# A ring of eleven buffers for the gathered expert rows of a kernel's last 256 tokens

## The chip, the core and the metric

The kernel runs on one core of a Trainium2 chip, as one launch. The metric is the device time of that launch in microseconds (us); lower is better. Engines are named as in the profile: PE is TensorE (PEld its weight loads), DVE is VectorE, ACT is ScalarE, POOL is GpSimd, SP is SyncE, whose queue issues the plain DMAs. Row gathers (indirect DMAs) are issued by POOL.

## The reference, cut to what matters

One decoder layer on 1024 tokens of width 1024: a token mixer with three branches, then a feed-forward layer that picks, for each token, 8 heads x 16 experts out of 16384, and a last norm. Only the expert layer bears on this change:

```
def chunk(xc):                                   # 128 tokens
    qh = (xc @ w_q).reshape(Ct, H, 2, PEER_QDIM // 2)
    s = jnp.einsum("nhad,akd->nhak", qh, sub_keys)
    top_s, top_i = lax.top_k(s, K)
...
    eidx = jnp.take_along_axis(cand_idx, pos, axis=-1)
    gate = jax.nn.softmax(best_s, axis=-1)
    ug = u_tab[eidx]
    vg = v_tab[eidx]
    hpre = jnp.einsum("nd,nhkd->nhk", xc, ug)
    act = gate * jax.nn.gelu(hpre, approximate=False)
    return jnp.einsum("nhk,nhkd->nd", act, vg)
```

So a token reads 128 rows of `u_tab` and 128 rows of `v_tab`, each of 1024 float32 numbers.

## The kernel before, in words

The 1024 tokens are cut into four parts of 256 (two tiles of 128 tokens each). All parts go through the mixer, the norm and the routing. Then the expert layer is computed in two ways.

Parts 1 and 2 (512 tokens) are done densely: 128 iterations, each for 128 experts, on PE. An iteration loads 512 KB of the u table (`uraw`) and 512 KB of the v table (`vraw`), splits both into two float16 halves (`us`, `vs`; high half on ACT, low half on DVE, line 212), multiplies the tokens with u (`g`, 24 matmuls, line 256), takes GELU, multiplies by the gates (`ge`, DVE line 1411), splits the result (`ac`, DVE line 212) and multiplies it with v (`acc`, 18 matmuls, line 1418; every fourth iteration 24 more into `g`). `gemm1` runs three iterations ahead.

Parts 0 and 3 (tiles 0, 1 and 6, 7) gather their rows instead, in `gather_tile`. For column c of a tile's 128 expert numbers, POOL issues one indirect DMA that brings one row for each of 128 tokens, a tile of 128 x 1024 float32 (512 KB), called `u6_5` for tile 6, column 5. DVE multiplies it with the normed tokens `gh2` and sums into column c of `hpre` (line 1144); 128 columns make the u phase of a tile. Then `act` is formed, and in the v phase each gathered `v` row is multiplied by its `act` column and added to `gacc` (line 1154), one after the other, since each addition reads the sum of the one before. Tiles 6 and 7 run beside the dense iterations, and what is left of them runs after these.

A gathered row sits in a buffer from its issue until DVE has used it. Tiles 0 and 1 use the tag `rows` alone, with RB = 5 buffers. `gather_tile` takes its own tiles from the same five: `gh2` for the whole u phase, `gacc` from shortly before the v phase to the end. So four of the five are left for rows. Tiles 6 and 7 (the last part) take their rows through `late_rows`, which goes round a ring of RB + 4 = 9 places: five from `rows`, then four that are the halves of two tiles of the tag `hT` (two buffers of 128 x 2 x 1024; they held the part's normed tokens, which are no longer needed by then). Such a half shows up under the name `rr_u` or `rr_v` in the profile, the other rows as `u` or `v`. A tile of `hT` comes free when both halves have been used. With nine places and eight free buffers, the fifth place of a round shares its buffer with the first of the same round.

The order of instructions on each engine is fixed when the kernel is built: a scheduler puts what is ready, by its own estimate, in order of priority, and each engine then runs its list in that order and waits where data is missing. A buffer that comes free at another moment therefore moves instructions on POOL, DVE, PE, ACT and SP.

The tag `o0`, `o1`, `o2` (pool `wk`, one buffer each) holds a part's three branch outputs. For the last part it also serves, through `WT`, the norm's rows, the top-16 lists `ts` (`o2`) and the one-hot tables of the routing (`oneh0` in `o0`, `oneh1` in `o1`, lines 1061 to 1066). The routing of tile 7 is still using `oneh0` and `oneh1` when tile 6 begins to gather.

Of the kernel before, what the change touches and what calls it, by code (L numbers as in the profile page):

```python
# [10 lines left out]
F32 = mybir.dt.float32  # L11
# [18 lines left out]
RB, WB, AT, ZB, TB = 5, 4, 8, 2, 3  # L30

T = 1024
D = 1024
# [36 lines left out]
def trunk(ctx: ExitStack, tc: tile.TileContext, a: dict, out: bass.AP):  # L70
# [11 lines left out]
    wk = ctx.enter_context(tc.tile_pool(name="wk", bufs=1))  # L82
# [988 lines left out]
    def rows(name):  # L1071
        return gat.tile([128, D], F32, tag="rows", name=name, bufs=RB)

    taken = [0, None]

    def late_rows(name):

        j = taken[0] % (RB + 4)
        taken[0] += 1
        if j < RB:  # L1080
            return rows(name)
        if (j - RB) % 2 == 0:
            taken[1] = htp.tile([128, 2, D], F32, tag="hT", name=f"rr_{name}")
        return taken[1][:, (j - RB) % 2]

    marks = []
    seen = [0]
# [459 lines left out]
```

## Time and profile before

| | us |
|---|---|
| median of 3 runs | 3650.54 |
| lowest, highest | 3646.55, 3655.01 |
| the profiled execution, its own time | 3644.86 |
| its span, first to last instruction | 3643.1 |

| stretch of the span, us | what runs |
|---|---|
| 2447 to 2743 | u phase of tile 6, beside dense iterations |
| 2743 to 3045 | v phase of tile 6, beside dense iterations |
| 3056 to 3340 | u phase of tile 7, beside dense iterations |
| 3341 to 3635 | v phase of tile 7; the last dense matmul ends at 3548 |

A row of the timeline gives start, duration, engine, line, operation, output <- inputs, a count, and in brackets the idle time of the engine just before it and what ended that. A row of the waits says who waited for whom, the sum, how often, and the longest. A row of the windows gives, for one stretch, the busy time of each engine (and its number of instructions), then the clock granted to PE, the busy share of the 16 DMA engines and the bytes moved per second. POOL's time for a gather is the time that it takes to issue it; the data lands later.

### The profile page before, as it was taken

To read this page: it belongs to the slowest core of one execution; us is meant where nothing else is said; L and a number is where in the kernel's file an instruction comes from. 1 tells how busy PE (TensorE), PEld (TensorE's weight loads), DVE (VectorE), ACT (ScalarE), POOL (GpSimd) and SP (SyncE) were. 2 spreads that over 40 slices of the span, in tenths; PEclk is the share of its full clock that TensorE was granted. 3 is DMA by queue.
4 is the path that set the end of the run, shared out by engine and by line. 5 is a ranking of instruction groups with operands and counts; after the bars stand their busy time and mean duration, and the time that the engine had idled before them with its cause. 6 is when DMAs were issued, how large, how long until landed. Compare 5 with 4: busy or idle time off the path is not lost.

```text
span 3643.1 us, 57457 instructions
## 1 busy us (share of the span) xinstructions
PE 3273.9 (90%) x20660; PEld 2192.5 (60%) x20660; DVE 3025.3 (83%) x7062; ACT 1594.5 (44%) x3162; POOL 1358.0 (37%) x1166
## 2 busy tenths in 40 slices
PE   7999999999987999999788889989999999999980
PEld 6887777777875778787566554534444444444430
DVE  6665689888899879889988777999988888997887
ACT  5776455553543564654456423243333333333311
POOL 0000002344332423332232334316665666775564
PEclk9999999999995889999576799999999999999995
DMA  8964857889976768987465899869999999999987
GB/s 303 340 223 142 297 189 253 306 293 345 349 258 199 260 227 297 333 307 253 135 228 179 294 365 314 288 192 357 366 359 321 347 331 353 383 377 340 335 281 249
DMA packets 358764, 1053.90 MB, mean 289 GB/s; under 512 B 35175, under 2 KB 107563, under 8 KB 354381
## 3 DMA queue, kind: packets, MB, share of 16 engines
q0 software_dynamic: 147456, 536.94, 41.8%
q1 hardware_dynamic: 211020, 513.29, 39.7%
q8 instruction: 162, 2.65, 0.3%
q14 instruction: 126, 1.02, 0.1%
HBM read 942.09 MB, written 108.00 MB: 288 GB/s over the span
## 4 chain that ended last, share of the span: by engine, by line
PE 37%; DVE 20%; DMA 16%; issue 13%; ACT 7%; POOL 6%; SPq 0%; POOLq 0%; DVEq 0%; ACTq 0%
DMA v<-in_peer_v_dram,gidx 7%; PE g L256 5%; PE pj_mg L256 4%; PE acc L1418 4%; POOL rr_v L1152 3%; DVE gacc L1154 3%; DMA d_G<-stage 3%; PE pj_r_hg L256 3%; POOL v L1152 2%; DVE u L1144 2%; DMA u<-in_peer_u_dram,gidx 2%; ACT stage L1217 2%; PE g L1418 2%; PE pj_wo L256 1%; DMA gt<-d_G 1%
## 5 line engine op out<-in xcount | busy, mean ns | idle before, releaser
L1152 POOL DMA_INDIRECT v<-in_peer_v_dram,gidx x398 | 518.6, 1303 | 731.3 <-DVE gacc L1154 447.5
L1142 POOL DMA_INDIRECT u<-in_peer_u_dram,gidx x399 | 488.7, 1225 | 676.9 <-DVE u L1144 398.4
L256 PE MATMUL g<-h,us 128*128 128x512 f16 x3072 | 695.0, 384 | 20.2 <-ACT p L1427 9.9
L1154 DVE SCALAR_TENSOR_TENSOR gacc<-v,act,gacc 128x1024 f32<-128x1024 f32 x398 | 508.9, 1279 | 115.7 <-DMA v<-in_peer_v_dram,gidx 112.8
L1418 PE MATMUL acc<-vs,ac 128*128 128x512 f16 x2304 | 536.3, 383 | 19.8 <-ACT ac L211 11.1
L1418 PEld LDWEIGHTS <-ac 128*128 128x128 f16 x3072 | 302.5, 99 | 398.9 <-issue 24.1
L256 PEld LDWEIGHTS <-us 128*128 128x128 f16 x3072 | 303.3, 99 | 392.1 <-issue 31.2
L1144 DVE SCALAR_TENSOR_TENSOR u<-u,gh 128x1024 f32<-128x1024 f32 x399 | 481.0, 1217 | 36.6 <-DMA u<-in_peer_u_dram,gidx 35.2
L256 PE MATMUL pj_mg<-hT,w_mg 128*128 128x256 f16 x2304 | 278.8, 277 | 12.4 <-ACT mg L884 6.5
L256 PEld LDWEIGHTS <-w_mg 128*128 128x128 f16 x2304 | 229.8, 101 | 43.3 <-issue 15.7
L1377 ACT ACTIVATE ge<-g 128x512 f32<-128x512 f32 x128 | 75.8, 592 | 367.5 <-PE g L256 360.7
L211 ACT ACTIVATE ac<-ge 128x512 f16<-128x512 f32 x128 | 80.0, 626 | 348.5 <-DVE ge L1411 313.4
L1152 POOL DMA_INDIRECT rr_v<-in_peer_v_dram,gidx x113 | 167.0, 1478 | 112.7 <-DVE gacc L1154 78.1
L1142 POOL DMA_INDIRECT rr_u<-in_peer_u_dram,gidx x113 | 168.3, 1490 | 96.8 <-DVE rr_u L1144 58.4
L211 ACT ACTIVATE vs<-vraw 128x1024 f16<-128x1024 f32 x128 | 133.3, 1046 | 139.6 <-DMA vraw<-in_peer_v_dram 139.5
L1418 PE MATMUL g<-vs,ac 128*128 128x512 f16 x768 | 178.4, 384 | 11.6 <-ACT ge L1377 8.8
L212 DVE SCALAR_TENSOR_TENSOR vs<-vraw,vs 128x1024 f16<-128x1024 f32 x128 | 155.7, 1219 | 20.0 <-ACT vs L211 19.5
L1217 ACT ACTIVATE stage<-gb 128x512 f32<-128x512 f32 x128 | 131.0, 1072 | 81.9 <-DMA d_G<-stage 40.4
L212 DVE SCALAR_TENSOR_TENSOR us<-uraw,us 128x1024 f16<-128x1024 f32 x128 | 155.9, 1218 | 7.9 <-ACT us L211 7.3
L256 PE MATMUL pb<-o,w_b 128*128 128x256 f16 x1152 | 142.7, 280 | 18.2 <-DMA w_b<-dw 9.9
L1214 PE MATMUL gb<-hot 128*128 128x128 f16 x512 | 126.3, 295 | 35.3 <-DVE hot L1211 20.8
L1411 DVE TENSOR_TENSOR ge<-ge,gt 128x256 f32<-128x256 f32 x256 | 98.1, 421 | 60.8 <-ACT ge L1377 30.3
(1145 smaller groups left out, 6556.7 us busy)
## 6 DMA issues: line engine op xcount, KB each, us to landing
uraw<-in_peer_uT_dram SPq DMA_DIRECT2D x128, 512.0 KB
vraw<-in_peer_v_dram SPq DMA_DIRECT2D x128, 512.0 KB
w_mg<-dw SPq DMA_DIRECT2D x72, 512.0 KB
d_G<-stage SPq DMA_DIRECT2D x32, 1024.0 KB
gt<-d_G SPq DMA_DIRECT2D x32, 1024.0 KB
w_r_hg<-dw SPq DMA_DIRECT2D x36, 512.0 KB
w_b<-dw SPq DMA_DIRECT2D x72, 256.0 KB
wr_mg<-in_wblk_dram SPq DMA_DIRECT2D x24, 512.0 KB
```

The source lines that it names most:

```text
L211: S.activation(hi, src, AF.Copy, scale=scale)
L212: V.scalar_tensor_tensor(lo, in0=src, scalar=scale, in1=hi, op0=ALU.mult, op1=ALU.subtract)
L256: P.matmul(ps, l[:, k, :], r[:, k, :], start=(i == 0), stop=(i == n - 1))
L1142: G.indirect_dma_start(out=ur, out_offset=None, in_=a["peer_u"], in_offset=bass.IndirectOffsetOnAxis(ap=idx[:, c:c + 1], axis=0))
L1144: V.scalar_tensor_tensor(ur, in0=ur, scalar=1.0, in1=h2, op0=ALU.mult, op1=ALU.mult, accum_out=hpre[:, c:c + 1])
L1152: G.indirect_dma_start(out=vr, out_offset=None, in_=a["peer_v"], in_offset=bass.IndirectOffsetOnAxis(ap=idx[:, c:c + 1], axis=0))
L1154: V.scalar_tensor_tensor(acc, in0=vr, scalar=act[:, c:c + 1], in1=acc, op0=ALU.mult, op1=ALU.add)
L1214: P.matmul(ps[:, n, :], hs[:, 0, :, n], hs[:, 2, :, n], start=True, stop=False)
L1217: S.activation(stage[0][:, :, m0:m0 + 4].rearrange("p i n -> p n i"), ps, AF.Copy, scale=SA / SGT)
L1377: S.activation(ge, ps, AF.Gelu, scale=1.0 / (SW * SH2))
L1411: V.tensor_tensor(gv, gv, gt[:, :, i % 8, :], op=ALU.mult)
L1418: P.matmul(ps, ac[:, x, t * 128:(t + 1) * 128], v[:, y, dh * 512:(dh + 1) * 512], start=start and n == 0, stop=stop and n == 2)
```

## The change

The ring of the last part gets eleven places, each with a buffer of its own: four of `rows` (RB - 1 instead of RB), the four halves of `hT` as before, and the three buffers `o0`, `o1`, `o2`, one row each. Nothing else is edited. Line numbers behind the edit grow by four (1144 becomes 1148, 1154 becomes 1158).

```diff
     def late_rows(name):
 
-        j = taken[0] % (RB + 4)
+        j = taken[0] % (RB + 6)
         taken[0] += 1
-        if j < RB:
+
+        j -= RB - 1
+        if j < 0:
             return rows(name)
-        if (j - RB) % 2 == 0:
+        if j >= 4:
+            return wk.tile([128, D], F32, tag=f"o{j - 4}", name=name, bufs=1)
+        if j % 2 == 0:
             taken[1] = htp.tile([128, 2, D], F32, tag="hT", name=f"rr_{name}")
-        return taken[1][:, (j - RB) % 2]
+        return taken[1][:, j % 2]
```

The scheduler turns this into other lists, from the start of tile 6 on. Three places follow; numbers at the end of a name are the scheduler's own.

First, POOL in the v phase of tile 7, about column 100. Before, column 97 is the fifth of its round and stands behind the four halves of `hT` that follow it in number:

```order
L1152 DMA rr_v7_98_36111<-in_peer_v_dram,gidx_7_35471 128x1024 x2
L1152 DMA rr_v7_100_36116<-in_peer_v_dram,gidx_7_35471 128x1024 x2
L1152 DMA v7_97_36108<-in_peer_v_dram,gidx_7_35471 128x1024
L1152 DMA v7_102_36121<-in_peer_v_dram,gidx_7_35471 128x1024
L1152 DMA v7_103_36124<-in_peer_v_dram,gidx_7_35471 128x1024
```

Now, the same place:

```order
L1156 DMA rr_v7_93_36116<-in_peer_v_dram,gidx_7_35481 128x1024 x2
L1156 DMA rr_v7_95_36121<-in_peer_v_dram,gidx_7_35481 128x1024 x2
L1156 DMA v7_97_36126<-in_peer_v_dram,gidx_7_35481 128x1024
L1156 DMA v7_98_36129<-in_peer_v_dram,gidx_7_35481 128x1024
L1156 DMA v7_99_36132<-in_peer_v_dram,gidx_7_35481 128x1024
L1156 DMA v7_100_36135<-in_peer_v_dram,gidx_7_35481 128x1024
```

The columns now stand in the order of their numbers, seven single rows and four halves in turn.

Second, DVE at the end of the dense part: `ac127` is the split of the last iteration's GELU, `vs126` and `vs127` those of its last v blocks, and `gacc_7<-v7_79` the use of column 79. Before:

```order
L212 SCALAR_TENSOR_TENSOR vs127_32985<-vraw127_32983,vs127_32985 128x1024
L1154 SCALAR_TENSOR_TENSOR gacc_7_35837<-v7_76_36049,act_7_35477,gacc_7_35837 128x1024
L1428 TENSOR_TENSOR acc7_22937<-acc7_22937,p7_123_4_32854 128x512
L1154 SCALAR_TENSOR_TENSOR gacc_7_35837<-v7_77_36052,act_7_35477,gacc_7_35837 128x1024
L1411 TENSOR_TENSOR ge127_32863<-ge127_32863,gt120_0_32624 128x256
L1411 TENSOR_TENSOR ge127_32863<-ge127_32863,gt120_16_32626 128x256
L1154 SCALAR_TENSOR_TENSOR gacc_7_35837<-v7_78_36055,act_7_35477,gacc_7_35837 128x1024
L212 SCALAR_TENSOR_TENSOR ac127_32990<-ge127_32863,ac127_32990 128x512
L1154 SCALAR_TENSOR_TENSOR gacc_7_35837<-v7_79_36058,act_7_35477,gacc_7_35837 128x1024
```

Now:

```order
L212 SCALAR_TENSOR_TENSOR ac127_32990<-ge127_32863,ac127_32990 128x512
L212 SCALAR_TENSOR_TENSOR vs125_32925<-vraw125_32923,vs125_32925 128x1024
L1158 SCALAR_TENSOR_TENSOR gacc_7_35851<-v7_101_36138,act_7_35487,gacc_7_35851 128x1024
L1158 SCALAR_TENSOR_TENSOR gacc_7_35851<-v7_102_36141,act_7_35487,gacc_7_35851 128x1024
L1158 SCALAR_TENSOR_TENSOR gacc_7_35851<-v7_103_36144,act_7_35487,gacc_7_35851 128x1024
L1158 SCALAR_TENSOR_TENSOR gacc_7_35851<-rr_v7_104_36147,act_7_35487,gacc_7_35851 128x1024 x2
L1158 SCALAR_TENSOR_TENSOR gacc_7_35851<-rr_v7_106_36152,act_7_35487,gacc_7_35851 128x1024 x2
L1158 SCALAR_TENSOR_TENSOR gacc_7_35851<-v7_108_36157,act_7_35487,gacc_7_35851 128x1024
L1158 SCALAR_TENSOR_TENSOR gacc_7_35851<-v7_109_36160,act_7_35487,gacc_7_35851 128x1024
L1158 SCALAR_TENSOR_TENSOR gacc_7_35851<-v7_110_36163,act_7_35487,gacc_7_35851 128x1024
L212 SCALAR_TENSOR_TENSOR vs126_32955<-vraw126_32953,vs126_32955 128x1024
L1158 SCALAR_TENSOR_TENSOR gacc_7_35851<-v7_111_36166,act_7_35487,gacc_7_35851 128x1024
```

The next row of that list is `vs127`, and the one behind it column 112. Behind `ac127` stood columns 79 to 127, 49 rows; now stand columns 101 to 127, 27 rows. The split `vs127`, ahead of column 76 before, is ahead of column 112 now.

Third, POOL at the end of the u phase of tile 6. Before:

```order
L1152 DMA rr_v6_3_35103<-in_peer_v_dram,gidx_6_34726 128x1024 x2
L1152 DMA rr_v6_5_35108<-in_peer_v_dram,gidx_6_34726 128x1024 x2
L1142 DMA u6_108_35033<-in_peer_u_dram,gidx_6_34726 128x1024
L1142 DMA u6_109_35036<-in_peer_u_dram,gidx_6_34726 128x1024
L1142 DMA u6_110_35039<-in_peer_u_dram,gidx_6_34726 128x1024
L1142 DMA u6_111_35042<-in_peer_u_dram,gidx_6_34726 128x1024
```

Now:

```order
L1156 DMA v6_6_35116<-in_peer_v_dram,gidx_6_34726 128x1024
L1156 DMA rr_v6_8_35122<-in_peer_v_dram,gidx_6_34726 128x1024 x2
L1146 DMA u6_107_35034<-in_peer_u_dram,gidx_6_34726 128x1024
L1146 DMA u6_97_35006<-in_peer_u_dram,gidx_6_34726 128x1024
L1146 DMA u6_118_35065<-in_peer_u_dram,gidx_6_34726 128x1024
L1146 DMA u6_108_35037<-in_peer_u_dram,gidx_6_34726 128x1024
L1156 DMA v6_1_35101<-in_peer_v_dram,gidx_6_34726 128x1024
L1146 DMA u6_119_35068<-in_peer_u_dram,gidx_6_34726 128x1024
```

Columns 97, 108 and 119 share the buffer `o1`, columns 107 and 118 `o0`: the first rows in `o0` and `o1` (columns 8 and 9) wait for the routing of tile 7 and are issued behind columns 38 and 49, and these two buffers stay behind until the phase ends, where they are used one row after the other.

## The prediction

> **What bounds the kernel now.** I read the page first, then the windows over the four phases of tiles 6 and 7, then the waits in them, then the timeline of the last 50 us.
>
> ```profile
> span 3643.1 us, 57457 instructions
> PE 3273.9 (90%) x20660; PEld 2192.5 (60%) x20660; DVE 3025.3 (83%) x7062; ACT 1594.5 (44%) x3162; POOL 1358.0 (37%) x1166
> ```
>
> The lists differ only from the start of tile 6 on, so the page's means say little; the stretches do. The windows below are the v phase of tile 6, the u phase of tile 7, the v phase of tile 7 beside the dense part, and what comes behind it. In each: length, then busy time of PE, PEld, DVE, ACT and POOL with their counts, the clock granted to PE, the DMA share and GB/s.
>
> ```profile
> 2757.00:3045.00 288.00, 285.45 (x1316) 129.02 (x1314) 247.23 (x263) 90.66 (x122) 172.66 (x118) 0.99 0.95 335
> 3060.00:3290.00 230.00, 227.46 (x1047) 102.67 (x1046) 211.55 (x344) 78.16 (x105) 169.04 (x112) 0.99 1.02 383
> 3350.00:3540.00 190.00, 181.31 (x829) 81.49 (x827) 156.69 (x167) 52.17 (x71) 113.35 (x80) 0.97 0.90 318
> 3540.00:3643.00 103.00, 8.29 (x39) 3.56 (x37) 75.92 (x89) 12.60 (x25) 52.57 (x43) 0.56 0.73 247
> ```
>
> Two things are to be seen. While dense iterations run, PE is busy 95 to 99% of the time, so that stretch can't shrink; the only time to win is the last 95 us, when PE is done and rows are still coming. And POOL issues a row each 230 / 112 = 2.05 us in the u phase of tile 7, but only each 288 / 118 = 2.44 and 190 / 80 = 2.38 us in the two v phases, with the DMA engines at 335 and 318 GB/s instead of 383. Why, the waits say: the first fence is the v phase of tile 6, the second the u phase of tile 7, the third and fourth the last two windows.
>
> ```profile
> POOL v L1152 <- DVE gacc L1154: 45.6, 14, 6.1
> POOL rr_v L1152 <- DVE gacc L1154: 45.4, 20, 5.5
> DVE gacc L1154 <- DMA v<-in_peer_v_dram,gidx: 37.6, 12, 5.3
> ```
>
> ```profile
> POOL rr_u L1142 <- DVE rr_u L1144: 21.3, 11, 5.8
> ```
>
> ```profile
> POOL v L1152 <- DVE gacc L1154: 34.5, 14, 5.7
> DVE gacc L1154 <- DMA v<-in_peer_v_dram,gidx: 26.7, 8, 5.2
> POOL rr_v L1152 <- DVE gacc L1154: 25.4, 11, 5.3
> ```
>
> ```profile
> DVE gacc L1154 <- DMA v<-in_peer_v_dram,gidx: 21.6, 6, 5.1
> POOL v L1152 <- DVE gacc L1154: 12.7, 5, 3.4
> POOL rr_v L1152 <- DVE gacc L1154: 7.2, 7, 2.0
> ```
>
> In the v phases POOL waits for a buffer that DVE has not emptied, and a little later DVE waits for a row that POOL issued too late. One round of the ring behind the dense part shows the loop:
>
> ```profile
> 3596.55 1.28 DVE L1154 SCALAR_TENSOR_TENSOR gacc<-v,act,gacc 128x1024 f32<-128x1024 f32 x1 [4.02 <-DMA v<-in_peer_v_dram,gidx]
> 3597.87 5.25 DVE L1154 SCALAR_TENSOR_TENSOR gacc<-rr_v,act,gacc 128x1024 f32<-128x1024 f32 x4
> ...
> 3600.75 1.86 POOL L1152 DMA_INDIRECT rr_v<-in_peer_v_dram,gidx  x1 [0.78 <-DVE gacc L1154]
> ...
> 3605.56 1.02 POOL L1152 DMA_INDIRECT rr_v<-in_peer_v_dram,gidx  x1 [0.30 <-issue]
> ...
> 3606.88 1.02 POOL L1152 DMA_INDIRECT v<-in_peer_v_dram,gidx  x1 [0.30 <-issue]
> ...
> 3613.54 1.28 DVE L1154 SCALAR_TENSOR_TENSOR gacc<-v,act,gacc 128x1024 f32<-128x1024 f32 x1 [5.13 <-DMA v<-in_peer_v_dram,gidx]
> ```
>
> DVE uses the fifth row of a round at 3596.55. After two halves of `hT` POOL may issue the next four halves (3600.75 to 3606.6), and behind them, at 3606.88, the next fifth row, which DVE uses at 3613.54, 6.66 us later. The round takes 3613.54 - 3596.55 = 17.0 us for nine rows, of which DVE works 9 x 1.31 = 11.8 (5.25 for four) and waits 5.1.
>
> **The change, part by part.** No arithmetic is added or removed: the same 512 rows, matmuls and splits. What moves is when a row is issued, and with it the lists. The base is the profiled execution, 3644.86 us with a span of 3643.1; the median of the runs is 5.7 us above it, and what I forecast is a difference, put on the median.
>
> *The end, behind the last split of the dense part.* The rows for it:
>
> ```profile
> 3537.84 0.68 DVE L212 SCALAR_TENSOR_TENSOR ac<-ge,ac 128x512 f16<-128x512 f32 x1
> ```
>
> ```profile
> L1447 DVE SCALAR_TENSOR_TENSOR yd<-acc,yd 128x512 f32<-128x512 f32 x8 | 5.5, 684 | 0.0
> L1449 DVE SCALAR_TENSOR_TENSOR yd<-yd,y_find,gfd 128x1024 f32<-128x1024 f32 x4 | 5.1, 1276 | 0.0
> L1428 DVE TENSOR_TENSOR acc<-acc,p 128x512 f32<-128x512 f32 x2 | 1.4, 680 | 0.0
> L229 DVE TENSOR_TENSOR u_find<-u_find,ms_find 128x1 f32<-128x1 f32 x4 | 0.6, 160 | 0.0
> ```
>
> ```profile
> L212 DVE SCALAR_TENSOR_TENSOR vs<-vraw,vs 128x1024 f16<-128x1024 f32 x14 | 17.0, 1217 | 0.0
> ```
>
> ```profile
> 3635.36 1.06 ACT L221 ACTIVATE sqf<-gacc 128x1024 f32<-128x1024 f32 x1 [62.70 <-DVE gacc L1154]
> ```
>
> Today the last split ends at 3538.5 and the program at 3643.1: 104.6 us for 49 rows. Now 27 rows are left there. With eleven buffers in order of number, a row is issued when the eleventh before it has been used, and DVE needs 11 x 1.31 = 14.4 us for eleven, more than issue and landing take (about 2 + 6.7), so rows no longer wait for landing and DVE sets the pace: 27 x 1.31 = 35.4; the three `vs` splits that now stand here, 3 x 1.22 = 3.7; the dense part's own finish, 5.5 + 5.1 + 1.4, and five kinds of tiny instruction at 0.6, 3.0; behind the last row, unchanged, 3643.1 - 3635.3 = 7.8. That is 61.9. The finish needs PE's last product, and PE starts it only behind `vs127`: 9.1 us of matmuls (an iteration's 3.88, and the 5.2 of every fourth; rows below), while DVE has four rows, 5.2 us, to do: a wait of 4. So 66 instead of 104.6: **-39** (between -46, if rows overlap at 1.2 us each and nothing waits, and -23, if rows still wait for landing half as much as now, 11 us, and PE twice as long).
>
> *The 22 rows that now come ahead of that split.* They cost 22 x 1.28 = 28.2 us of DVE if nothing hides them, nothing if they fill its waits for landing, 37.6 + 26.7 = 64.3 us. Sixteen fall into the last 16 iterations (91 rows there instead of 75): DVE would be busy (156.7 + 16 x 1.2) / 190 = 93% of that window, POOL 96 x (1.42 + 0.30) = 165 of 190 us, and the DMA engines would move 318 + 16 x 0.524 MB / 190 us = 362 GB/s. The u phase of tile 7 had all three at once, 92%, 1.81 us per issue and 383 GB/s, with PE at 99%. The window lies at that edge, where a late row holds up the `ac` and `vs` splits queued behind it on DVE, and PE with them. I take **+6** (0 to +28).
>
> *The end of tile 6's u phase.* The `o1` rows 97, 108 and 119 come one after the other, each only when DVE has used the one before, and `act` waits for the last; the v rows are queued behind on POOL, the splits on DVE, and PE behind these.
>
> ```profile
> 3064.85 8.10 DMA u<-in_peer_u_dram,gidx
> ...
> 3220.73 5.18 PE g L256 x24
> 3225.91 3.88 PE acc L1418 x18
> ...
> 3262.17 5.18 PE g L256 x24
> ```
>
> One such trip is an issue of 1.51 us (169.04 / 112), a landing of 8.1 and a use of 1.28: 10.9 us. Two trips lie between the use of column 97 and `act`, 22 us. The dense splits that the list has between them are about 2.7 iterations' worth, and an iteration takes PE (3262.17 - 3220.73) / 4 = 10.4 us, so PE has 28 us of work there: nearly hidden. **+4** (0 to +15). SP's list moves as well: the load of `gacc` for tile 6 stands four iterations earlier, and the `uraw` and `vraw` loads behind it wait while it waits for a buffer, about a row's 2 us, which the three iterations that `gemm1` leads cover.
>
> Sum: -39 + 6 + 4 = **-29**, so 3615.9 against 3644.9, or 3650.5 - 29 = 3621.5.
>
> **The Trainium skill against it.** The first row is the start of tile 6, to be held against the four above.
>
> ```profile
> 2440.00:2500.00 60.00, 56.52 (x249) 25.01 (x249) 54.80 (x122) 23.48 (x32) 32.59 (x27) 0.94 0.83 293
> ```
>
> An issue took 32.59 / 27 = 1.21 us with DVE 91% busy, 1.22 with DVE 74% busy at the end, 1.51 where the DMA engines were full: it goes by the DMA load and not by DVE. The Trainium skill, "SBUF — State Buffer", section "SBUF: two separate sides", says that GpSimd cannot write the descriptors of its DMAs while DVE runs an operation that takes the shared port pair. By that rule a DVE at 93% would hold up the issues and rows would come no faster than today, which is the first rival's time; these rows do not show it for this kernel's operations.
>
> **The rivals.** *Rows come no faster, and the splits wait for them (slower).* The lists now put 22 more rows ahead of the last split. If a row still takes 2.4 us in the v phases, because the DMA share there, 0.95, is already near full, DVE stands at these rows with the dense splits behind it: 22 x 2.4 = +53, with the end's -39, +14: 3664.5. It turns from a gain to a loss where a moved row costs the dense part more than 35 / 22 = 1.6 us. For it: 0.95 busy at only 335 GB/s. Against: the share falls to 0.90 and 0.73 where POOL waits longest, and 383 GB/s were moved beside a full PE. 12%.
>
> *The trips of `o1` stop PE (no change).* If DVE gets no dense split done in three trips, they cost 3 x 10.9 = 33 instead of 4, and -29 becomes 0: 3650.5. For it: each list is fixed, and the stop comes at a point where PE has no slack. Against: the splits stand between the rows. 13%. This is also the way in which the change would not do what it says: in this phase two of the eleven buffers are late.
>
> *Everything fits.* The 22 rows are hidden wholly, the trips too, and the end is at its best: -46, 3604.5. Against it: DVE, POOL and the DMA engines would all have to run above what the u phase of tile 7 showed. 13%.
>
> **How the numbers follow.** The forecast (62%) is 3621.5; its own range is 3605 to 3640. 3602 to 3655 takes in the last two rivals and most of the unknown costs, and leaves out the slower rival and the ends that add up all the worst terms. No change means within 0.2%, 7.3 us, about what a measurement of this kernel can tell. Faster: the forecast and the best case, 75%, and a little of the second rival, 77%; the same 12%; slower 11%.
>
> **What would show it.** Right: POOL at about 2.1 us a row in the v phases, its waits for `gacc` under half, the DMA engines above 355 GB/s there, 27 rows behind the last split and 66 us from it to the end, dense matmuls ending some 10 us later than 3548. Wrong: PE with new waits for `ac` or `vs` splits of tens of us, a last dense matmul behind 3580, or POOL still at 2.4 us a row.

## The result, and the profile after

The changed kernel takes 3593.48 us (median of 4 runs, 3589.78 to 3599.18) against 3652.78 us for the kernel before (4 runs beside them). The ratio is 0.984, with a 95% interval of 0.9815 to 0.9864: 59 us less, where the forecast was 29 less and the low end of the range, 3602, 48.5 less. The profiled execution took 3591.76 us. Its page begins:

```profile
span 3590.0 us, 57440 instructions
PE 3274.6 (91%) x20660; PEld 2193.6 (61%) x20660; DVE 3023.9 (84%) x7062; ACT 1596.5 (44%) x3160; POOL 1358.2 (38%) x1166
```

The work of every engine is the same. The same stretches as before (the third ends 10 us earlier, and the fourth runs from there to the new end):

```profile
2757.00:3045.00 288.00, 288.00 (x1336) 130.51 (x1335) 271.97 (x295) 101.36 (x134) 184.55 (x133) 1.00 0.99 369
3060.00:3290.00 230.00, 230.00 (x1067) 104.25 (x1066) 207.01 (x333) 72.74 (x97) 163.00 (x108) 1.00 1.00 370
3350.00:3530.00 180.00, 164.69 (x748) 73.52 (x747) 168.65 (x174) 51.73 (x69) 123.63 (x89) 0.98 0.97 361
3530.00:3590.00 60.00, 21.83 (x88) 9.06 (x87) 53.03 (x73) 12.07 (x25) 22.04 (x21) 0.72 0.69 261
```

In the v phase of tile 6 POOL issues a row each 288 / 133 = 2.17 us (before 2.44), in that of tile 7 each 180 / 89 = 2.02 (before 2.38), and the DMA engines move 369 and 361 GB/s (before 335 and 318). DVE is busy 94% of both (before 86% and 82%). The waits in the first of these stretches say why:

```profile
POOL rr_v L1156 <- DVE gacc L1158: 23.5, 15, 2.5
POOL v L1156 <- DVE gacc L1158: 22.6, 21, 4.2
...
DVE gacc L1158 <- DMA v<-in_peer_v_dram,gidx: 1.4, 1, 1.4
```

POOL waits half as long for DVE to empty a buffer (46.1 us, before 91.0), and DVE has all but stopped waiting for rows (1.4, before 37.6).

The clearest account is that of DVE from the first row of tile 6 to the end of the program. The first two rows are the windows of before, cut at the end of the last `ac` split; the next two those of after.

```profile
2447.76:3538.50 1090.74, 1069.64 (x4915) 482.79 (x4914) 958.27 (x1315) 349.94 (x470) 681.30 (x472) 0.99 0.96 346
3538.50:3643.00 104.50, 9.79 (x46) 4.23 (x44) 76.20 (x90) 12.60 (x25) 53.39 (x44) 0.56 0.73 248
```

```profile
2452.07:3531.90 1079.83, 1059.23 (x4880) 478.28 (x4879) 983.03 (x1336) 352.26 (x468) 708.37 (x496) 0.99 0.97 360
3531.90:3590.00 58.10, 20.06 (x81) 8.25 (x79) 51.13 (x71) 12.07 (x25) 20.51 (x20) 0.71 0.68 259
```

DVE's work is the same to 0.3 us (958.3 + 76.2 = 1034.5, and 983.0 + 51.1 = 1034.2). So the time from tile 6 on is this work and what DVE stands idle: 160.8 us before, 103.8 after. The 57.0 us of difference are the gain; that tile 6 starts 4.3 us later, where the lists are still the same, takes the profiled difference to 53.1. The same sum comes out for PE, whose work is as constant (1079.4 and 1079.3 us, idle 115.8 and 58.6): it tells how much waiting went, and not yet which engine sets the time. What DVE waited for over the whole stretch, before and then after:

```profile
DVE gacc L1154 <- DMA v<-in_peer_v_dram,gidx: 84.9, 26, 5.3
DVE ge L1411 <- DMA gt<-d_G: 25.2, 9, 5.5
DVE ge L1411 <- ACT ge L1377: 15.1, 10, 2.9
...
DVE vs L212 <- ACT vs L211: 4.4, 4, 2.1
```

```profile
DVE ge L1415 <- ACT ge L1381: 42.4, 26, 5.2
DVE vs L212 <- ACT vs L211: 25.2, 14, 8.2
DVE acc L1432 <- ACT p L1431: 9.9, 5, 5.6
...
DVE ge L1415 <- DMA gt<-d_G: 2.3, 2, 1.6
...
DVE gacc L1158 <- DMA v<-in_peer_v_dram,gidx: 1.4, 1, 1.4
```

Waits for rows (with 6.2 us in the u phases, 91.1 before) fall to 1.4, those for `gt` by 23. In their place DVE waits more for the dense part: for the GELU, and so for PE (+27), for `vs` blocks (+21) and for `p` (+9). Of 113 us saved (89.7 and 22.9) half is given back there. The part of `gt` is not needed for the gain: in spread9, below, DVE waits 35.4 us for `gt`, 10 more than before, and the time is as short.

### The profile page after: what moved, and what is told of

It is laid out like the page before. It is cut to its first block, busy times and chain, and to the rows that moved or that the text cites. A ratio compares the mean times of both kernels' runs of the same rounds, so it can differ in the third digit from the quotient of the medians.

```text
span 3590.0 us, 57440 instructions
## 1 busy us (share of the span) xinstructions
PE 3274.6 (91%) x20660; PEld 2193.6 (61%) x20660; DVE 3023.9 (84%) x7062; ACT 1596.5 (44%) x3160; POOL 1358.2 (38%) x1166
## 3 DMA queue, kind: packets, MB, share of 16 engines
q14 instruction: 125, 1.02, 0.1%
## 4 chain that ended last, share of the span: by engine, by line
PE 50%; DVE 22%; DMA 12%; issue 7%; ACT 7%; POOL 2%; SPq 0%; DVEq 0%; POOLq 0%; ACTq 0%
PE g L256 11%; PE acc L1422 9%; PE pj_mg L256 4%; DVE gacc L1158 4%; PE g L1422 3%; PE pj_r_hg L256 3%; DVE u L1148 3%; DMA v<-in_peer_v_dram,gidx 2%; DMA d_G<-stage 2%; PE pb L256 2%; DMA u<-in_peer_u_dram,gidx 2%; PE pj_wo L256 2%; DMA gt<-d_G 1%; DMA vraw<-in_peer_v_dram 1%; ACT stage L1221 1%
## 5 line engine op out<-in xcount | busy, mean ns | idle before, releaser
L1156 POOL DMA_INDIRECT v<-in_peer_v_dram,gidx x421 | 559.4, 1329 | 699.5 <-DVE gacc L1158 411.7
L1146 POOL DMA_INDIRECT u<-in_peer_u_dram,gidx x417 | 524.6, 1258 | 692.9 <-DVE u L1148 380.8
L1422 PE MATMUL acc<-vs,ac 128*128 128x512 f16 x2304 | 540.5, 383 | 34.5 <-ACT vs L211 13.8
L1158 DVE SCALAR_TENSOR_TENSOR gacc<-v,act,gacc 128x1024 f32<-128x1024 f32 x421 | 537.7, 1277 | 30.5 <-DMA v<-in_peer_v_dram,gidx 27.5
L1148 DVE SCALAR_TENSOR_TENSOR u<-u,gh 128x1024 f32<-128x1024 f32 x417 | 501.4, 1216 | 31.4 <-DMA u<-in_peer_u_dram,gidx 30.9
L1146 POOL DMA_INDIRECT rr_u<-in_peer_u_dram,gidx x95 | 135.2, 1424 | 79.0 <-DVE rr_u L1148 58.0
L1156 POOL DMA_INDIRECT rr_v<-in_peer_v_dram,gidx x90 | 123.6, 1374 | 71.0 <-DVE gacc L1158 43.8
```

Of the source, the lines that this page charges most:

```text
L1146: G.indirect_dma_start(out=ur, out_offset=None, in_=a["peer_u"], in_offset=bass.IndirectOffsetOnAxis(ap=idx[:, c:c + 1], axis=0))
L1148: V.scalar_tensor_tensor(ur, in0=ur, scalar=1.0, in1=h2, op0=ALU.mult, op1=ALU.mult, accum_out=hpre[:, c:c + 1])
L1156: G.indirect_dma_start(out=vr, out_offset=None, in_=a["peer_v"], in_offset=bass.IndirectOffsetOnAxis(ap=idx[:, c:c + 1], axis=0))
L1158: V.scalar_tensor_tensor(acc, in0=vr, scalar=act[:, c:c + 1], in1=acc, op0=ALU.mult, op1=ALU.add)
L1422: P.matmul(ps, ac[:, x, t * 128:(t + 1) * 128], v[:, y, dh * 512:(dh + 1) * 512], start=start and n == 0, stop=stop and n == 2)
```

## The experiments

The diff changes two things at once: it adds three buffers (`o0`, `o1`, `o2`), and it takes away the fifth place of `rows`, which shared its buffer with the first. The forecast rested on the number of buffers. The first experiments undo that part in steps. The table sums up all runs; "distance" is the least number of columns between two rows that use one buffer (a tile of `hT` comes free with its second half), "landing" the time that DVE waits for rows from tile 6 on, "idle" all of DVE's idle time there (from the profiled execution of each).

| kernel | places / buffers | distance | rows behind last `ac` | landing, us | idle, us | median, us | ratio to before, 95% interval |
|---|---|---|---|---|---|---|---|
| before | 9 / 8 | 4, once in nine | 49 | 91.1 | 160.8 | 3652.8 | 1 |
| after | 11 / 11 | 10 | 27 | 1.4 | 103.8 | 3593.5 | 0.9840, 0.9815 to 0.9864 |
| ring8 | 8 / 8 | 7 | 43 | 1.0 | 100.6 | 3588.0 | 0.9825, 0.9804 to 0.9846 |
| ring9 | 9 / 9 | 8 | 43 | 0.2 | 93.2 | 3595.5 | 0.9856, 0.9833 to 0.9879 |
| ring10 | 10 / 10 | 9 | 41 | 3.3 | 103.2 | 3585.3 | 0.9828, 0.9804 to 0.9851 |
| spread9 | 9 / 8 | 7 | 44 | 9.0 | 101.2 | 3586.7 | 0.9831, 0.9806 to 0.9856 |
| ring6 | 6 / 8 | 6, for the four of `rows` | 46 | 47.1 | 124.1 | 3616.3 | 0.9907, 0.9884 to 0.9930 |
| ring4 | 4 / 4 | 4 | 49 | 209.2 | 243.1 | 3736.2 | 1.0228, 1.0200 to 1.0257 |
| t7_only | tile 6 as before, tile 7 as after | 4, then 10 | 40 | 44.7 | 122.9 | 3610.2 | 0.9881, 0.9854 to 0.9907 |
| after_fifth | 12 / 11 | 4, once in twelve | 51 | 35.4 | 142.2 | 3641.5 | 0.9971, 0.9952 to 0.9991 |
| late_o01 | 9, then 11 | 8, then 10 | 37 | 0.3 | 98.5 | 3586.2 | 0.9827, 0.9802 to 0.9852 |
| r8_gidx2 | 8 / 8 | 7 | 43 | 1.3 | 99.8 | 3581.0 | 0.9799, 0.9772 to 0.9825 |
| gidx2 | 11 / 11 | 10 | 25 | 0 | 111.1 | 3592.0 | 0.9842, 0.9813 to 0.9871 |
| after_again | 11 / 11 | 10 | 27 | 0 | 104.6 | 3591.4 | 0.9849, 0.9821 to 0.9877 |

### Fewer buffers, each place with its own

**ring8**

```diff
-        j = taken[0] % (RB + 6)
+        j = taken[0] % (RB + 3)
```

> Eight places, each with a buffer of its own: four of rows and the four halves of hT, no o0, o1, o2. That is as many buffers as before had, but the columns stand in order of their numbers. The list has 43 rows behind the last ac split (before 49, after 27). Theory 'depth' (what counts is how many rows are in flight; with eight the eleventh-before rule fails and rows are waited for as before): DVE still waits some 70 to 90 us for landing between the start of tile 6 and the end (before 91, after 1.4), and only the six rows fewer behind the split are won, 6 x 1.3 = 8 us: about 3643. Theory 'order' (what cost the time was the fifth place, which shares its buffer with the first and stands late on POOL): the waits for landing fall under 30 us and the time is after's plus 16 rows more behind the split, 16 x 1.28 = 20: about 3614.

Measured: 3588.0 us. The whole gain is there with the eight buffers that the kernel before had. Two fences: its windows from tile 6's first row, cut at the end of the last `ac` split, and DVE in its tail.

```profile
2450.32:3508.20 1057.88, 1055.44 (x4882) 478.00 (x4881) 965.76 (x1323) 350.70 (x470) 676.64 (x477) 1.00 0.98 360
3508.20:3585.00 76.80, 16.36 (x76) 7.22 (x74) 68.35 (x83) 12.48 (x25) 44.55 (x39) 0.64 0.82 300
```

```profile
3560.45 5.25 DVE L1158 SCALAR_TENSOR_TENSOR gacc<-rr_v,act,gacc 128x1024 f32<-128x1024 f32 x4
3565.73 5.25 DVE L1158 SCALAR_TENSOR_TENSOR gacc<-v,act,gacc 128x1024 f32<-128x1024 f32 x4
3571.01 2.61 DVE L1158 SCALAR_TENSOR_TENSOR gacc<-rr_v,act,gacc 128x1024 f32<-128x1024 f32 x2
```

Eight rows take 3571.01 - 3560.45 = 10.56 us, 1.32 each: DVE alone sets the pace, where a round of before took 17.0 us for nine, 1.89 each. Theory "depth" is refuted. Theory "order" has the cause on its side, but its number, 3614, was 26 too high: it charged the 16 rows that stand behind the split as an addition. They are none. The last split comes 1057.9 us after tile 6's first row (after: 1079.8), and behind it the program takes 76.8 (after: 58.1). Rows that DVE does not do behind the dense part it does beside it, and 965.8 + 68.4 is the same 1034 us.

**ring9** and **ring10**: the same with nine and ten.

```diff
-        j = taken[0] % (RB + 6)
+        j = taken[0] % (RB + 4)
...
-            return wk.tile([128, D], F32, tag=f"o{j - 4}", name=name, bufs=1)
+            return wk.tile([128, D], F32, tag="o2", name=name, bufs=1)
```

```diff
-        j = taken[0] % (RB + 6)
+        j = taken[0] % (RB + 5)
...
-            return wk.tile([128, D], F32, tag=f"o{j - 4}", name=name, bufs=1)
+            return wk.tile([128, D], F32, tag=f"o{j - 3}", name=name, bufs=1)
```

> Nine places with nine buffers: ring8 and o2. 43 rows behind the last ac split, as with eight. Theory 'depth': half way on the chip's side, landing waits of 40 to 60 us: about 3632. Theory 'order': as with eight, about 3614, no difference to ring8 above the uncertainty.

> Ten places: ring8, o0 and o1 (o2 stays out). 41 rows behind the last ac split, and one vs split. Theory 'depth': landing waits of 10 to 25 us, about 3616. Theory 'order': about 3611, two rows less than ring8.

Measured: 3595.5 and 3585.3 (the ten places are ring8, `o1` and `o2`; the expectation names `o0` and `o1`). From eight places to eleven the intervals all overlap, and DVE waits under 4 us for rows in each. The number of buffers, from eight up, buys nothing that can be measured.

### The shared place, or the distance

What ring8 leaves open is whether the ninth place was bad because it had no buffer of its own, or because its buffer's former row stood only four columns ahead.

**spread9**, an edit of the kernel before:

```diff
-        if j < RB:
+        if j % 2 == 0:
             return rows(name)
-        if (j - RB) % 2 == 0:
+        if j % 4 == 1:
             taken[1] = htp.tile([128, 2, D], F32, tag="hT", name=f"rr_{name}")
-        return taken[1][:, (j - RB) % 2]
+        return taken[1][:, j // 2 % 2]
```

> The nine places and eight buffers of before, five of rows and four halves of hT, but in turn: row, half, row, half, and so on, a row last. Only the order of the places differs from before. A fifth row still shares its buffer with the first of its round, but now a row is issued into a buffer whose former row stands seven or eight columns back; before, the fifth place stands only four columns behind the first. 44 rows behind the last ac split. Theory 'distance' (what counts is the shortest distance in columns between two rows of one buffer): as ring8 or a few us above, 3590 to 3598, with under 15 us of waits for landing on DVE from the start of tile 6. Theory 'place' (a ninth place without a buffer of its own is the cost, wherever it stands): no gain but for the rows behind the split, 3640 to 3650, with 70 us of waits or more.

Measured: 3586.7 us, 3 below the range that "distance" gave, with nine places on the same eight buffers. What is left of its waits for rows in the v phases:

```profile
DVE gacc L1154 <- DMA v<-in_peer_v_dram,gidx: 6.3, 6, 1.5
```

84.9 us of waits in 26 stops have become 6.3 in six. Theory "distance" holds and "place" falls: nothing but the order in which the same places are taken, with the lists that the scheduler makes of it, was worth the whole gain.

**ring6** and **ring4** shorten the distance with no place shared.

```diff
-        j = taken[0] % (RB + 6)
+        j = taken[0] % (RB + 1)
```

```diff
-        j = taken[0] % (RB + 6)
+        j = taken[0] % (RB - 1)
```

> Six places with six buffers: four of rows and the two halves of one hT tile in turn. The shortest distance is five columns (a tile of hT is free when its second half has been used). 46 rows behind the last ac split. Theory 'distance': behind the dense part a round of six takes 6 x 1.28 = 7.7 us of DVE against about 1.4 of issue and 6.7 of landing and a turn, so DVE waits 2 to 3 us a round, eight rounds, about 20; beside the dense part a row comes each 2.2 us, 13 us for six, and little is waited: 3608 to 3625. Theory 'place': six tidy places are like eight, 3588 plus three rows, 3592.

> Four places, the rows alone: distance four everywhere. 49 rows behind the last ac split, as before. Theory 'distance': each fourth row has to wait for an issue of 1.4, a landing of 7 to 8 and a turn, some 9.5 us for four rows of 5.1 us: 12 rounds behind the dense part x 4.4 = 53 us, and beside it, where four rows take DVE about 9 us with the dense work between, some 0 to 2 us in each of 115 rounds: 3700 to 3850. Theory 'place': a small loss against ring8, under 3620, since no place is shared.

Measured: 3616.3 and 3736.2, both within what "distance" gave and far from "place". (The expectation miscounts ring6: the two tiles of `hT` serve in turn, so its halves are far apart, and only the four buffers of `rows` come back after six columns.) The waits of ring6, then of ring4; in ring6 they are all at `u` and `v`, the rows of the near buffers, and none at `rr_u` or `rr_v`:

```profile
DVE u L1148 <- DMA u<-in_peer_u_dram,gidx: 23.8, 22, 3.2
DVE gacc L1158 <- DMA v<-in_peer_v_dram,gidx: 23.3, 23, 2.6
```

```profile
DVE u L1148 <- DMA u<-in_peer_u_dram,gidx: 107.8, 86, 3.7
DVE gacc L1158 <- DMA v<-in_peer_v_dram,gidx: 101.4, 92, 3.5
```

The tails give the length of the loop (use, issue, landing, use) itself. In ring4:

```profile
3680.52 5.25 DVE L1158 SCALAR_TENSOR_TENSOR gacc<-v,act,gacc 128x1024 f32<-128x1024 f32 x4 [3.19 <-DMA v<-in_peer_v_dram,gidx]
3687.31 1.28 DVE L1158 SCALAR_TENSOR_TENSOR gacc<-v,act,gacc 128x1024 f32<-128x1024 f32 x1 [1.54 <-DMA v<-in_peer_v_dram,gidx]
3689.85 2.61 DVE L1158 SCALAR_TENSOR_TENSOR gacc<-v,act,gacc 128x1024 f32<-128x1024 f32 x2 [1.25 <-DMA v<-in_peer_v_dram,gidx]
3692.97 2.61 DVE L1158 SCALAR_TENSOR_TENSOR gacc<-v,act,gacc 128x1024 f32<-128x1024 f32 x2 [0.52 <-DMA v<-in_peer_v_dram,gidx]
3696.71 1.28 DVE L1158 SCALAR_TENSOR_TENSOR gacc<-v,act,gacc 128x1024 f32<-128x1024 f32 x1 [1.13 <-DMA v<-in_peer_v_dram,gidx]
```

Nine rows take 3696.71 - 3680.52 = 16.2 us, 1.80 each, so a loop of four takes 7.2 us, of which DVE works 4 x 1.31 = 5.2. In ring6 the first and the last of 18 rows, with little else between:

```profile
3567.79 5.25 DVE L1158 SCALAR_TENSOR_TENSOR gacc<-v,act,gacc 128x1024 f32<-128x1024 f32 x4 [1.05 <-DMA v<-in_peer_v_dram,gidx]
...
3594.45 2.61 DVE L1158 SCALAR_TENSOR_TENSOR gacc<-v,act,gacc 128x1024 f32<-128x1024 f32 x2
```

(3594.45 - 3567.79) / 18 = 1.48 us a row, a loop of six in 8.9, of which DVE works 7.9. At 1.31 us a row a loop of 7.2 to 8.9 us is covered by 5.5 to 6.8 columns: six (ring6) is a little short, seven (spread9, and the halves in ring8) enough.

### The short place, put back

**after_fifth** is the changed kernel with one more place, on the old shared buffer.

```diff
-        j = taken[0] % (RB + 6)
+        j = taken[0] % (RB + 7)
         taken[0] += 1
 
-        j -= RB - 1
+        j -= RB
```

> The changed kernel with the fifth place of rows put back: twelve places in turn (five of rows, four halves, o0, o1, o2) on the same eleven buffers, so that again the fifth place shares its buffer with the first, four columns ahead. 51 rows behind the last ac split (after 27, before 49). Theory 'distance': one row in twelve is four columns behind its buffer's former row, where before it was one in nine: 91 x 9 / 12 = 68 us of DVE waits for landing, and by the runs so far each us of these costs 0.6 to 0.7 us: 3588 + 0.65 x 68 = 3632 (3625 to 3640). Theory 'number of buffers': as after, 3591, or 24 rows x 1.28 = 31 above it for the list alone, 3622, with waits under 15 us.

Measured: 3641.5 us. With eleven buffers, three more than ring8, one short distance in twelve takes back 48 of the 59 us. "Number of buffers" is refuted a second time. The sizes came out differently from what I worked out: 35 us of waits for rows and not 68, and the median 1.5 above my range (the profiled execution took 3630.8). DVE's largest waits ahead of the last split are others:

```profile
DVE vs L212 <- ACT vs L211: 40.3, 14, 7.9
DVE ge L1415 <- ACT ge L1381: 39.7, 22, 4.0
DVE gacc L1158 <- DMA v<-in_peer_v_dram,gidx: 22.4, 11, 4.3
```

As I read it, the scheduler sees the short place too and puts rows later (51 behind the last split), so that DVE has fewer rows to fill its waits for the dense part with. Against the changed kernel's profile, though, most of the added idle time is waiting for rows: 34.0 us (35.4 and 1.4) of 38.4 (142.2 and 103.8), while the waits for `vs` grew by 15 and others fell. What share of the loss lies in these lists, and what in waits on the chip, I could not separate: each change of a buffer changes both.

### One tile alone, and the `o` buffers later

**t7_only** gives the eleven places to tile 7 alone, and starts the count of places anew with each tile. The diff is cut: `ring9_rows` and `ring11_rows` are `late_rows` of before and of after.

```diff
...
-        row = late_rows if ti // 2 == PARTS[-1].i else rows
+        row = (ring11_rows if ti == 7 else ring9_rows) if ti // 2 == PARTS[-1].i else rows
+        taken[0] = 0
```

> Tile 6 gathers through the old nine places, tile 7 through the eleven. 40 rows behind the last ac split, three vs splits (as after). Theory 'end' (the gain is that of the rows which no longer stand behind the dense part, with their waits, and tile 6 matters little): after's time plus 13 rows x 1.28 = 17, about 3610. Theory 'all along' (each us that DVE doesn't wait in tile 6 is handed on to tile 7, so half of the gain is made there): about 3622 to 3628, with PE again losing some 9 us where tile 6 ends.

Measured: 3610.2 us, the number of theory "end". But DVE's waits, up to 3060 us, show that tile 6 is not indifferent:

```profile
DVE gacc L1169 <- DMA v<-in_peer_v_dram,gidx: 37.6, 12, 5.7
```

From there to the end DVE waits 2 us for rows. All that is left of the waits is tile 6's, 43 us, and the idle time is 19 us above after's, as is the median (3610.2 against 3591 to 3593). By that, about a third of the gain is made in tile 6; the theories' numbers were too near each other to say more.

**late_o01** keeps `o0` and `o1` out of tile 6's u phase, and with them the trips of columns 97, 108 and 119.

```diff
-        j = taken[0] % (RB + 6)
+        if taken[0] < 128:
+            j = taken[0] % (RB + 4)
+            j = RB + 5 if j == RB + 3 else j
+        else:
+            j = (taken[0] - 128) % (RB + 6)
```

> The changed kernel, but o0 and o1 join the ring only from the v phase of tile 6 on; its u phase goes round nine places (four rows, four halves, o2). So the trips of columns 97, 108 and 119 through one buffer are gone. 37 rows behind the last ac split, two vs splits. Theory 'trips cost little' (mine, 4 us, by which the dense splits hide them): within 8 us of after's 3591. Theory 'trips stop DVE' (22 to 33 us): 3560 to 3570, since these come off.

Measured: 3586.2 us; its interval overlaps that of after. In the changed kernel column 97 is used at 2744.0 us and column 119 at 2762.8, so that the two trips between them take 18.8 us (22 forecast). The window around them has PE busy throughout:

```profile
2724.00:2770.00 46.00, 46.00 (x215) 20.84 (x213) 29.38 (x42) 20.28 (x25) 10.82 (x10) 1.00 0.65 224
```

The trips cost PE nothing there. The medians are 5 to 7 us apart, which the intervals don't tell from nothing.

### The gap between the tiles

Between tile 6's last row and tile 7's first POOL stands still, since the list of expert numbers has one buffer:

```profile
3028.76 0.94 POOL L1146 DMA_INDIRECT u<-in_peer_u_dram,gidx  x1 [22.21 <-DVE ac L212]
```

**r8_gidx2** (on ring8) and **gidx2** (on the changed kernel) give it two:

```diff
-        idx = load(gat.tile([128, 128], I32, tag="gidx", name=f"gidx_{ti}", bufs=1), d_idx[ti])
-        gate = load(gat.tile([128, 128], F32, tag="ggate", name=f"ggate_{ti}", bufs=2), d_gate[ti])
+        idx = load(gat.tile([128, 128], I32, tag="gidx", name=f"gidx_{ti}", bufs=2), d_idx[ti])
+        gate = load(gat.tile([128, 128], F32, tag="ggate", name=f"ggate_{ti}", bufs=1), d_gate[ti])
```

> ring8, with two buffers for gidx (and one for ggate, to make room), so that the list of expert numbers of tile 7 can be loaded before tile 6's last row is issued. POOL stands 22 us without an issue between the two tiles in the changed kernel. 43 rows behind the last ac split, as in ring8. Theory 'DVE has other work there' (no row is waited for at that place): no difference to ring8, 3588 within 6 us. Theory 'gap' (POOL's idle time is handed on to the end): 3566 to 3575.

> The changed kernel with the same two buffers for gidx. 25 rows behind the last ac split instead of 27. Theory 'DVE has other work there': two rows, 3 us, 3588. Theory 'gap': 3570.

Measured: 3581.0 and 3592.0. This does not settle theory "gap", since the second buffer moves POOL's idle time and does not remove it. In gidx2 POOL issues tile 7's first rows from 3008.1 us on, but waits soon after, until the last use of tile 6's `gacc`:

```profile
3047.21 1.68 POOL L1146 DMA_INDIRECT u<-in_peer_u_dram,gidx  x1 [20.60 <-DVE gacc L1163]
```

From 2980 to 3060 us POOL is idle for 39.2 us in the changed kernel and 40.3 in gidx2, for 39.0 in ring8 and 37.1 in r8_gidx2. What that idle time is worth stays open. 3581.0 is the lowest median of all, but its interval overlaps ring8's, so I claim no gain of its own for the second buffer.

**after_again**, the changed kernel on the chip of spread9, ring6 and ring4:

> The changed kernel itself, on the same chip as the three others, to be held against ring8's 3588: the theories that count places expect it faster than eight places by 5 to 15 us, those that count distance within 8 us, since DVE waits for a row for under 2 us in both.

Measured: 3591.4 us, ratio 0.9849 (0.9821 to 0.9877), so ring8's 0.9825 (0.9804 to 0.9846) is not told apart from it, as "distance" has it.

## Why the prediction was wrong, point by point

**Most signs came, the size didn't.** POOL at 2.17 and 2.02 us a row (2.1 forecast), over 355 GB/s, 27 rows behind the last split, the last dense matmul about 10 us later. Two signs came otherwise. From the last split to the end it took 58 us and not 66. And POOL's waits for `gacc`, forecast at under half, were 46.1 of 91.0 us in tile 6's v phase and 38.8 of 59.9 in tile 7's (up to 3530 us):

```profile
POOL v L1156 <- DVE gacc L1158: 23.5, 21, 2.6
POOL rr_v L1156 <- DVE gacc L1158: 15.3, 10, 3.5
```

One sign of being wrong came in part: PE has 23.2 us of new waits for `vs` splits (13.8 and 9.4, shown below), though its last dense matmul is not behind 3580. The last `ac` split on DVE and the end of the dense part on PE, in the changed kernel:

```profile
3531.24 0.68 DVE L212 SCALAR_TENSOR_TENSOR ac<-ge,ac 128x512 f16<-128x512 f32 x1
...
3547.37 5.26 PE L1422 MATMUL acc<-vs,ac 128*128 128x512 f16 x12 [6.71 <-DVE vs L212]
...
3557.22 1.46 PE L1422 MATMUL acc<-vs,ac 128*128 128x512 f16 x6
```

The dense part ends at 3558.7, and PE waited 6.7 us for `vs126`, which stands behind ten rows in DVE's list, but DVE had these rows to do meanwhile.

**Term 1, the end, -39: measured -46.4** (104.5 to 58.1), the term's best bound. DVE's work there fell by 76.2 - 51.1 = 25.1 and its idle time by 21.3 (28.3 to 7.0), which is the 21.6 of waits for rows. The step was right; the wait of 4 for PE's last product was 0.4, and a row took 1.2 rather than 1.31 where another instruction stands between.

**Terms 2 and 3, the rows ahead of the split and the `o1` trips, +6 and +4: measured -10.9** (1090.7 to 1079.8 from tile 6's first row to the split). This is the step that failed, by 21 us. The prediction set 64.3 us of waits for rows against 28.2 us of added rows, and used the waits only as cover: "(0 to +28)". What was left, 36 us, it dropped, because PE was busy 95 to 99% and "that stretch can't shrink". But the stretch ends with a split in DVE's list, and DVE had idle time to give: in the measured stretch its work rose by 24.8 and its idle time fell by 35.7, from 132.5 to 96.8. PE's idle time there hardly changed (21.1 and 20.6 us), but 10.3 us of its work moved behind the split (9.79 and 20.06 in the rows of the two ends), beside DVE's rows.

Nor is PE's share a floor at 95%. In the kernel before, splits stood in DVE's list behind rows that were late, and PE waited for them. DVE and then PE, just ahead of the last split:

```profile
3520.70 1.28 DVE L1154 SCALAR_TENSOR_TENSOR gacc<-v,act,gacc 128x1024 f32<-128x1024 f32 x1 [4.92 <-DMA v<-in_peer_v_dram,gidx]
...
3528.26 0.68 DVE L212 SCALAR_TENSOR_TENSOR ac<-ge,ac 128x512 f16<-128x512 f32 x1
```

```profile
3529.00 11.53 PE L1418 MATMUL acc<-vs,ac 128*128 128x512 f16 x40 [8.69 <-DVE ac L212]
```

A row is 4.92 us late, the split behind it ends at 3528.9, and PE has stood 8.69 us for it. The last dense matmuls, before and then in ring8:

```profile
3546.84 1.46 PE L1418 MATMUL acc<-vs,ac 128*128 128x512 f16 x6
```

```profile
3523.11 1.46 PE L1422 MATMUL acc<-vs,ac 128*128 128x512 f16 x6
```

Before, they end 1100.5 us after tile 6's first row; in ring8 1074 us after it. In ring9 and spread9 PE waits for nothing in that time, and it takes 1070. Of the 31 us between before and spread9, 21 are waits of PE; the rest is that the same matmuls were busy for 1069.8 us and not 1079.4, at a granted clock of 1.00 and not 0.99.

In the changed kernel that gain is hidden, and its dense matmuls end 1106.6 us after tile 6's first row, since its list puts rows ahead of the `vs` splits and PE waits for these:

```profile
PE acc L1422 <- ACT vs L211: 13.8, 5, 7.5
PE acc L1422 <- DVE vs L212: 9.4, 4, 6.7
```

To carry the 36 us over whole would have been too much: -39 - 36 + 4 = -71, 12 more than came, since DVE's other waits took part of it back.

**The mechanism, in part wrong.** The prediction saw the loop of the fifth place (17.0 us a round, 5.1 of it waiting) and yet argued from the number: eleven buffers give 14.4 us. By the same sum eight give 8 x 1.31 = 10.5, more than the 8.7 it set against them. What the change did of use is `RB - 1`; the three `o` buffers, which bring the ring to eleven, and their trips are worth nothing measurable.

**The rivals.** "Rows come no faster" did not come: they come faster with DVE busier. "The trips stop PE" did not come (46.00 of 46 us). "Everything fits" (3604.5) was nearest, and still 11 too slow, because it too let the dense stretch keep its length.

**The rule that speaks against it.** The prediction held a rule of the Trainium skill, "SBUF — State Buffer", section "SBUF: two separate sides", against itself: with it a DVE at 93% would hold up POOL's issues, which gives the first rival's time. The Trainium skill, in that section, says so of a DVE instruction in a 2-port performance mode; for one with two SBUF inputs, as line 1158 has, it names a lock only against a GpSimd instruction that reads SBUF. The prediction did not make that difference. This case's rows show no hold-up by line 1158. The same 100 us of tile 6's v phase, before and after:

```profile
2850.00:2950.00 100.00, 100.00 (x465) 45.30 (x464) 87.32 (x93) 31.79 (x44) 61.75 (x42) 1.00 0.96 333
```

```profile
2850.00:2950.00 100.00, 100.00 (x465) 45.33 (x464) 96.00 (x99) 32.05 (x43) 70.01 (x49) 1.00 1.02 376
```

With DVE 87% busy POOL issued 42 rows at 1.47 us each, with DVE 96% busy 49 at 1.43. And where the Trainium skill, "Perfetto Trace Analysis", section "Optimization Strategy", says that the same gap in each round can mean there isn't enough SBUF for the next tile, spread9 shows the other reading: the gaps of before went away with the same eight buffers, taken in another order.

## What to carry to other kernels

In a ring of buffers look for the shortest distance between two uses of one buffer, not for the number of buffers: it has to cover issue and landing (here 7.2 to 8.9 us, seven rows of 1.31), and more than that buys nothing. When two engines are both busy nine tenths of the time, neither share need be a floor: take the work and the idle time of each from the first changed instruction to the end, and ask what each wait is for. Waits in the middle count too, though here less than those at the end: ahead of the last split the waits for rows fell from 69.5 us to 1.4 and DVE's idle time by 35.7, behind it they fell from 21.6 to nothing and the idle time by 21.3. Waits that a change removes are not only cover for what it adds: carry the surplus into the sum, less what other waits take back.

## What the runs showed of the hardware that I had not expected

- Against ring8, a microsecond more of waiting for rows went with 0.5 to 0.7 us of time, over a wide range: (3610.2 - 3588.0) / (44.7 - 1.0) = 0.51 in t7_only, (3616.3 - 3588.0) / (47.1 - 1.0) = 0.61 in ring6, (3652.8 - 3588.0) / 90.1 = 0.72 before, (3736.2 - 3588.0) / 208.2 = 0.71 in ring4. after_fifth lies outside it, with 53.5 / 34.4 = 1.56.
- DVE's chain of rows runs at 1.31 us a row (5.25 for four) although one instruction is 1.28.
- Gathers and dense loads together held 360 GB/s from tile 6's start to the last split, and 376 GB/s with PE at full speed beside them for 100 us, the DMA share at 1.02.
- Tile 6's first row is issued at 2447.8 us before, 2452.1 after and 2460.4 in ring10, though nothing ahead of it was edited: this spread is as large as the differences between the rings of eight to eleven.
